# Moving the high and low parts of x from byte 288 to byte 384 of their 512-byte blocks in SBUF

## The chip, the cores and the metric

The kernel runs on one core of one Trainium2 chip. The metric is device time in microseconds (us), taken as the median of several runs; one further execution was recorded by the hardware profiler.

## What is computed

Two layers of a gated mixer over 256 rows of width 2048, in float32. Cut to what matters here:

```python
def _layer(x, norm_g, w_in, w_out):             # both layers have this frame
    h = matmul(_rmsnorm(x, norm_g), w_in)       # (256 x 2048) @ (2048 x 8192)
    q, k, v, z = split(h)
    y = attention(rope(q), rope(k), v) * silu(z)
    return x + matmul(y, w_out)                 # (256 x 2048) @ (2048 x 2048)

out = _rmsnorm(layer_1(layer_0(x)), final_norm)
```

Layer 0 uses dilated and differential attention, layer 1 block-sparse attention. Nearly all the work is in the four projections.

## The kernel before, in words

**Arithmetic.** Every float32 operand of a projection is held as two tiles of type float32r: a high part h (a copy by ScalarE) and a low part l = value - h (by VectorE). A product is then three matmuls, h*h, h*l and l*h. Each TensorE matmul is preceded by a load of its 128x128 stationary operand; the moving operand streams through with 256 or 512 columns.

**The tiles of x.** `xhl` (L63) is a list of 16 tiles, one for each 128 rows of the transposed activations. A tile is 128 partitions by 2048 bytes: 1024 bytes of high parts followed by 1024 bytes of low parts, 256 columns each. `split_x` (L159, writes at L162 and L163) fills it: once at the start from the input, and once after layer 0 from PSUM (`next_x`, L421).

**Where they lie.** Tiles are allocated one behind the other in SBUF, at the same byte offset in every partition. The pool `edge` comes first and begins 128 bytes past a multiple of 512. It holds a pad of PAD bytes, the 16 tiles of x (each a multiple of 512 bytes long), and a second pad of BACK bytes:

```python
    edge = ctx.enter_context(tc.tile_pool(name="edge", bufs=1))
    edge.tile([P, PAD // 4], F32, name="pad")
    xhl = [edge.tile([P, 2, S], F32R, name=f"x{i}") for i in range(KT)]
    edge.tile([P, BACK // 4], F32, name="pad2")
```

The pads are never read or written. With PAD = 160 every tile of x begins at 288 past a multiple of 512. PAD and BACK add up to 384, so all that is allocated behind begins at a multiple of 512: the weights' raw loads (`raw`), their split halves (`wh`, `wl`), the gated outputs (`yh`, `yl`), q, k, v and the rest. Every 128-column, 256-column or 512-column slice of a matmul operand in those tiles therefore begins at a multiple of 512, and every slice of x at 288 past one.

**The order of the work.** The loop at L505 goes through chunks, two layers of four groups and then the output projection. In a group the chunks q, k and z are 256 output columns wide, and v is 512 wide. It issues one matmul after another, and between them `fill` holds the attention steps for fixed slots. There are three forms of projection matmul:

- **q, k, z** (L529, L531): x is the moving operand and the weights are stationary. A pair is one matmul of 512 columns (high and low parts of x at once, against `wh`) and one of 256 columns (high part of x against `wl`).
- **v** (L523, through `mm3`, L312): x is the stationary operand, and `wh` or `wl` move with 512 columns.
- **output projection** (L523, through `mm3`, L312): `yh` or `yl` is stationary, and `wh` or `wl` move with 512 columns. No tile of x takes part.

```python
                        nc.tensor.matmul(ps[:, b], wh[ww][:, bs], xx, start=first, stop=False,
                                         skip_group_check=True)
                        nc.tensor.matmul(ps[:, b, 0:S], wl[ww][:, bs], xx[:, 0:S], start=False, stop=final,
                                         skip_group_check=True)
```

**The last chunk** (`last_chunk`, L443, matmuls at L462) is the last quarter of the output projection of layer 1. Four of its eight weight blocks were split into the tiles of x, which are free by then (L117 to L119), so there x tiles hold weights and move: with 512 columns for the first 128 rows, with 256 columns for the second 128 rows, against stationary `yh` and `yl`.

**Weights.** `load` (L91) brings a 1 MB raw block on SyncE's DMA queue; `split` (L111) makes `wh` on ScalarE (L133) and `wl` on VectorE (L134), some blocks ahead of their use.

Of the kernel before, what the change touches and what calls it, by code (L numbers as in the profile page):

```python
# [26 lines left out]
RAW_BUFS = 3  # L27
SPLIT_BUFS = 4
ALIGN = 512
PAD = 160  # L30
BACK = 224


def layer_chunks():
# [21 lines left out]
def trunk(ctx, tc, x_nat, x_t, w0, o0, w1, o1, g0, g1, gfin, lam, subln, cos_t, sin_t,  # L56
# [4 lines left out]
# [4 lines that stand above are left out]
    const = ctx.enter_context(tc.tile_pool(name="const", bufs=1))  # L65
# [569 lines left out]
```

## Time and profile before

| | |
|---|---|
| median of 3 runs | 958.21 us (958.12 to 958.51) |
| profiled execution, its own time | 958.89 us |
| its span, first to last instruction | 957.1 us |
| TensorE (PE) busy | 946.3 us, 99% of the span |
| weight loads (PEld) busy | 819.1 us, 86% |
| VectorE (DVE) busy | 639.3 us, 67% |
| ScalarE (ACT) busy | 526.3 us, 55% |
| HBM | 184 GB/s over the span |

PE is TensorE streaming a moving operand; PEld is the load of a stationary operand, which runs beside it. Matmuls are pipelined: the duration of one in the trace (about 390 ns for 512 columns) is longer than the time until the next one starts. What a matmul costs the kernel is the distance between starts, called its pitch here. It is read from the start times in the timeline, or from a stretch of uninterrupted matmuls divided by their number.

### The profile page before, as it was taken

To read this page: it belongs to the slowest core of one execution; us is meant where nothing else is said; L and a number is where in the kernel's file an instruction comes from. 1 tells how busy PE (TensorE), PEld (TensorE's weight loads), DVE (VectorE), ACT (ScalarE), POOL (GpSimd) and SP (SyncE) were. 2 spreads that over 40 slices of the span, in tenths; PEclk is the share of its full clock that TensorE was granted. 3 is DMA by queue.
4 is the path that set the end of the run, shared out by engine and by line. 5 is a ranking of instruction groups with operands and counts; after the bars stand their busy time and mean duration, and the time that the engine had idled before them with its cause. 6 is when DMAs were issued, how large, how long until landed. Compare 5 with 4: busy or idle time off the path is not lost.

```text
span 957.1 us, 13108 instructions
## 1 busy us (share of the span) xinstructions
PE 946.3 (99%) x5132; PEld 819.1 (86%) x5132; DVE 639.3 (67%) x973; ACT 526.3 (55%) x807; POOL 6.0 (1%) x12
## 2 busy tenths in 40 slices
PE   8999999999999999999999999999999999999996
PEld 7888888888888888888888898888889888888886
DVE  6778678557856785655566787685678567755572
ACT  7556556445645564454544665564566455644451
POOL 0000000000000000000000000000000000000000
PEclk9999999999999999999999999999999999999999
DMA  9775454445554554544555544545454545554542
GB/s 327 247 295 181 146 190 176 169 175 195 185 173 162 196 179 175 176 176 176 181 176 203 190 169 156 203 155 194 164 191 170 182 173 180 191 205 176 181 171 88
DMA packets 27854, 177.09 MB, mean 185 GB/s; under 512 B 3344, under 2 KB 4112, under 8 KB 7696
## 3 DMA queue, kind: packets, MB, share of 16 engines
q1 hardware_dynamic: 27504, 175.21, 51.5%
q10 hardware_dynamic: 288, 1.05, 0.4%
q8 instruction: 40, 0.66, 0.3%
q14 instruction: 22, 0.18, 0.1%
HBM read 174.15 MB, written 2.10 MB: 184 GB/s over the span
## 4 chain that ended last, share of the span: by engine, by line
PE 96%; issue 1%; DMA 1%; SPq 0%; ACT 0%; DVE 0%; POOL 0%; POOLq 0%; ACTq 0%
PE acc L529 36%; PE acc L312 34%; PE acc L531 19%; PE ps_s L312 1%; PE last L462 1%; PE ps_t L352 1%; DMA raw<-in_w 1%; PE po L312 1%; PE ps_s L317 1%; PE po L383 1%; PE pdo L312 0%; PE ps_xt L426 0%; PE ps_yt L409 0%; SPq L99 0%; SPq L150 0%
## 5 line engine op out<-in xcount | busy, mean ns | idle before, releaser
L134 DVE TENSOR_TENSOR wl<-raw,wh 128x1024 fp32r<-128x1024 f32 x314 | 384.3, 1224 | 244.7 <-ACT wh L133 242.2
L529 PE MATMUL acc<-x,wh 128*128 128x512 f32 x1536 | 541.1, 393 | 0.0
L133 ACT ACTIVATE wh<-raw 128x1024 fp32r<-128x1024 f32 x314 | 332.3, 1059 | 292.5 <-PE acc L529 138.4
L531 PE MATMUL acc<-x,wl 128*128 128x256 f32 x1536 | 432.8, 282 | 0.0
L529 PEld LDWEIGHTS acc<-x,wh 128*128 128x128 f32 x1536 | 288.5, 188 | 58.4
L531 PEld LDWEIGHTS acc<-x,wl 128*128 128x128 f32 x1536 | 290.2, 189 | 0.3
L312 PE MATMUL acc<-wh,x 128*128 128x512 f32 x512 | 164.8, 400 | 1.6 <-ACT wh L130 1.6
L312 PEld LDWEIGHTS acc<-wh,x 128*128 128x128 f32 x512 | 96.9, 189 | 24.8 <-ACT wh L130 1.8
L312 PE MATMUL acc<-wl,x 128*128 128x512 f32 x256 | 101.9, 398 | 0.5 <-DVE wl L134 0.2
L312 PE MATMUL acc<-wh,yh 128*128 128x512 f32 x224 | 88.4, 394 | 0.0
L312 PE MATMUL acc<-wh,yl 128*128 128x512 f32 x224 | 87.3, 390 | 0.0
L312 PE MATMUL acc<-wl,yh 128*128 128x512 f32 x224 | 87.2, 389 | 0.0
L312 PEld LDWEIGHTS acc<-wl,x 128*128 128x128 f32 x256 | 48.5, 190 | 12.6 <-DVE wl L134 0.7
L312 PEld LDWEIGHTS acc<-wh,yl 128*128 128x128 f32 x224 | 42.0, 188 | 9.0
L312 PEld LDWEIGHTS acc<-wl,yh 128*128 128x128 f32 x224 | 42.1, 188 | 8.3
L312 PEld LDWEIGHTS acc<-wh,yh 128*128 128x128 f32 x224 | 42.1, 188 | 8.3
L326 ACT ACTIVATE p<-p,st 128x128 f32<-128x128 f32 x64 | 28.5, 448 | 9.9 <-DVE st L322 9.6
L375 ACT ACTIVATE yh<-y 128x256 fp32r<-128x256 f32 x32 | 13.0, 417 | 34.4 <-DVE y L374 34.3
L290 DVE TENSOR_TENSOR rt<-rt,sr 128x512 f32<-128x512 f32 x32 | 22.1, 690 | 3.7 <-ACT rt L288 2.4
L287 ACT ACTIVATE rt<-rt 64x512 f32<-64x512 f32 x32 | 20.2, 631 | 7.7 <-DVE rt L286 7.0
L286 DVE TENSOR_TENSOR rt<-acc,rt 128x512 f32<-128x512 f32 x32 | 21.8, 683 | 0.1
L288 ACT ACTIVATE rt<-rt 64x512 f32<-64x512 f32 x32 | 20.2, 632 | 0.4
(131 smaller groups left out, 646.9 us busy)
## 6 DMA issues: line engine op xcount, KB each, us to landing
raw<-in_w SPq DMA_DIRECT2D x124, 1024.0 KB, 4.7
raw<-in_o SPq DMA_DIRECT2D x32, 1024.0 KB, 4.7
raw<-in_w SPq DMA_DIRECT2D x7, 512.0 KB, 8.7
xraw<-in_x_t SPq DMA_DIRECT2D x8, 256.0 KB, 7.7
x_sb<-in_x_nat SPq DMA_DIRECT2D x1, 2048.0 KB, 11.0
out<-x_sb SPq DMA_DIRECT2D x8, 256.0 KB, 2.5
gf<-in_gfin ACTq DMA_DIRECT2D x2, 512.0 KB, 4.5
raw<-in_w SPq DMA_DIRECT2D x2, 256.0 KB, 4.5
```

Source lines behind the costliest of these rows:

```text
L133: nc.scalar.activation(ht, r, AF.Copy)
L134: nc.vector.tensor_sub(lt, r, ht.bitcast(F32))
L286: nc.vector.tensor_add(t1, ps[:, :, 0:S], t1)
L287: nc.scalar.activation(t2[0:64], t1[64:128], AF.Copy)
L288: nc.scalar.activation(t2[64:128], t1[0:64], AF.Copy)
L290: nc.vector.tensor_mul(t2, t2, sr[:, None, :].to_broadcast([P, 2, S]))
L312: nc.tensor.matmul(out_, l, r, start=start and i == 0, stop=stop and i == 2)
L317: nc.tensor.matmul(ps[:, 0:P], q[:, h, 0:P], k[:, h, 0:P], start=True, stop=True)
L326: nc.scalar.activation(p[:, sl], p[:, sl], AF.Exp, bias=st[:, 0, i:i + 1], scale=-1.0, accum_out=st[:, 1, i:i + 1])
L375: nc.scalar.activation(yh[kt], y, AF.Copy)
L529: nc.tensor.matmul(ps[:, b], wh[ww][:, bs], xx, start=first, stop=False, skip_group_check=True)
L531: nc.tensor.matmul(ps[:, b, 0:S], wl[ww][:, bs], xx[:, 0:S], start=False, stop=final, skip_group_check=True)
```

## The change

The two pads change their sizes; their sum stays 384 bytes. The 16 tiles of x move up by 96 bytes, from 288 to 384 past a multiple of 512. Nothing else moves, and no instruction is added or removed.

```diff
 ALIGN = 512
-PAD = 160
-BACK = 224
+PAD = 256
+BACK = 128
```

## Rows read from the trace of the kernel before

**Rows 1.** The page: TensorE's busy time, and its granted clock in 40 slices.

```profile
PE 946.3 (99%) x5132; PEld 819.1 (86%) x5132; DVE 639.3 (67%) x973; ACT 526.3 (55%) x807; POOL 6.0 (1%) x12
...
PEclk9999999999999999999999999999999999999999
```

**Rows 2.** The page: the chain that ended last, by engine.

```profile
PE 96%; issue 1%; DMA 1%; SPq 0%; ACT 0%; DVE 0%; POOL 0%; POOLq 0%; ACTq 0%
```

**Rows 3.** What TensorE waited for: us in total, times, longest us.

```profile
PE acc L312 <- ACT wh L130: 1.6, 1, 1.6
PE pw L148 <- DVE fs L450: 1.1, 1, 1.1
PE acc L312 <- DVE wl L134: 0.2, 1, 0.2
```

**Rows 4.** Costliest groups: line, engine, operation, out<-in, shapes, xcount | busy us, mean ns | idle before.

```profile
L529 PE MATMUL acc<-x,wh 128*128 128x512 f32 x1536 | 541.1, 393 | 0.0
L531 PE MATMUL acc<-x,wl 128*128 128x256 f32 x1536 | 432.8, 282 | 0.0
L312 PE MATMUL acc<-wh,x 128*128 128x512 f32 x512 | 164.8, 400 | 1.6 <-ACT wh L130 1.6
L312 PE MATMUL acc<-wl,x 128*128 128x512 f32 x256 | 101.9, 398 | 0.5 <-DVE wl L134 0.2
...
L133 ACT ACTIVATE wh<-raw 128x1024 fp32r<-128x1024 f32 x314 | 332.3, 1059 | 292.5 <-PE acc L529 138.4
```

**Rows 5.** Chain that ended last, in order of time: start us, us, what. v chunks, then output projection.

```profile
15.08 16.83 PE acc L312 x71
...
269.93 22.40 PE acc L312 x96
...
440.82 4.13 PE acc L312 x18
...
873.91 53.08 PE acc L312 x234
```

**Rows 6.** Timeline of PE, q/k/z just after a v chunk, then settled: start us, us, instruction.

```profile
292.16 0.40 PE L529 MATMUL acc<-x,wh 128*128 128x512 f32 x1
292.40 0.28 PE L531 MATMUL acc<-x,wl 128*128 128x256 f32 x1
292.51 0.40 PE L529 MATMUL acc<-x,wh 128*128 128x512 f32 x1
...
293.22 0.39 PE L529 MATMUL acc<-x,wh 128*128 128x512 f32 x1
...
300.18 0.39 PE L529 MATMUL acc<-x,wh 128*128 128x512 f32 x1
300.41 0.28 PE L531 MATMUL acc<-x,wl 128*128 128x256 f32 x1
...
302.26 0.39 PE L529 MATMUL acc<-x,wh 128*128 128x512 f32 x1
```

**Rows 7.** Timeline of PE in the last chunk: x tiles moving, then wh and wl moving.

```profile
929.62 0.63 PE L462 MATMUL last<-x,yh 128*128 128x512 f32 x2
...
931.02 0.63 PE L462 MATMUL last<-x,yh 128*128 128x512 f32 x2
...
938.25 0.40 PE L462 MATMUL last<-x,yh 128*128 128x256 f32 x2
...
939.30 0.39 PE L462 MATMUL last<-x,yh 128*128 128x256 f32 x2
...
942.02 0.28 PE L462 MATMUL last<-wh,yl 128*128 128x256 f32 x1
...
943.10 0.28 PE L462 MATMUL last<-wh,yl 128*128 128x256 f32 x1
```

**Rows 8.** Line L162, ScalarE's writes into the x tiles: duration ns min/median/max, first and last start.

```profile
L162 ACT ACTIVATE x<-xraw,g_sb x16: 489/495/509, 3.8 to 21.7; 128x256 fp32r<-128x256 f32 x16
L162 ACT ACTIVATE x<-ps_xt,g_sb x16: 458/474/476, 418.7 to 492.1; 128x256 fp32r<-128x256 f32 x16
```

## The prediction

> **What bounds the kernel now.** I read the page first, for who is busy: TensorE 99% of the span, at full granted clock in all 40 slices (2.4 GHz) [rows 1]. Then the chain that ended last: 96% of it is TensorE [rows 2]. Then what TensorE waited for: about 3 us in all, none of it after the start [rows 3]. So the kernel is a row of matmuls without gaps, and its time is the sum of their pitches, the distances between starts. Whatever the change does to a pitch reaches the end one for one; whatever it does to another engine is worth nothing as long as that engine keeps ahead, and ScalarE sat idle 292.5 us before its weight splits, most of it waiting for TensorE [rows 4].
>
> The pitch is therefore what to read, by the position of x. At 2.4 GHz 512 columns alone would stream in 213.3 ns and 256 in 106.7 ns. All operands but the tiles of x begin at multiples of 512 bytes, so the trace before already holds matmuls with x and without it:
>
> - **x stationary, weights moving, 512 columns (v).** One whole v chunk is 96 matmuls in 22.40 us, 233.3 ns each [rows 5].
> - **No x, 512 columns (output projection).** 234 matmuls in 53.08 us, 226.8 ns each; the short piece of 18 in 4.13 us gives 229.4, since the first few after an interruption are slower [rows 5].
> - **x moving, 512 columns, alone (last chunk).** Six starts in 1.40 us (929.62 to 931.02), 233.3 ns each [rows 7].
> - **x moving, 256 columns, alone (last chunk).** Nine in 1.05 us, 116.7 ns each; with `wh`, `wl` moving nine take 1.08 us, 120.0 ns each [rows 7].
> - **x moving in pairs of 512 and 256 (q, k, z).** Six pairs from 300.18 to 302.26, 346.7 ns a pair, split as 0.23 and 0.12 [rows 6]. Just after a v chunk a pair takes longer: three from 292.16 to 293.22 are 353.3 ns each, and then it settles [rows 6].
>
> So the same shape costs 233.3 ns where one operand is an x tile, on either side, and 226.8 ns where both operands begin at a multiple of 512: 6.5 ns more for 213.3 ns of columns. In the pairs that cost does not show: 346.7 is the sum of the two forms without x, 226.8 + 120.0 = 346.8. A pitch thus depends on where the operands begin, and it can sit at a slow value or settle to a fast one.
>
> **The change part by part.** Only the start of the 16 x tiles moves, from 288 to 384. Instructions, order, waits, DMAs and all other addresses stay. No matmul, semaphore or queue entry is added or taken away.
>
> *v, 768 matmuls (512 + 256 in [rows 4]).* No row has a tile at 384. The nearest from below is the output projection, 226.8 ns; from above today's 233.3 ns; a value still worse is bounded by the slowest steady row of this shape, 233.3 too. I take 226.8: 288 is a multiple of 32 only, while 384 is a multiple of 128 as is every start of the fast form, and the likeliest cause of 6.5 ns at 288 is a read that starts off such a boundary. Seven chunks run without a gap: 672 x 6.5 = 4.4 us. The first chunk is held by its loads until 15.08; from there 71 matmuls take 16.83 us, 237.0 ns each [rows 5], which gives up to 71 x 6.5 = 0.5 us and perhaps nothing. I take 4.5 us saved for v, with ends 0 and 4.9.
>
> *q, k, z, 1536 pairs [rows 4].* Here x moves. The nearest row for an aligned pair is the sum of the aligned forms, 346.8 ns against 346.7: I take no change. Below, a pair could reach 226.8 + 116.7 = 343.5 (the 256-column part at its best), 1536 x 3.2 ns = 4.9 us saved; above, 353.3, the pair just after a v chunk, 1536 x 6.6 ns = 10.1 us lost. This is the largest unknown: one nanosecond a pair is 1.5 us.
>
> *Last chunk.* 24 matmuls of 512 columns would gain 24 x 6.5 = 0.16 us, 48 of 256 columns would lose up to 48 x 3.3 = 0.16 us: nothing.
>
> *Writes into the x tiles.* 32 on ScalarE at 458 to 509 ns [rows 8], as many on VectorE. If a write at 384 took 5% more or less, 25 ns, it would stay hidden behind the matmuls, which run on; without that cover 64 x 25 ns = 1.6 us. Zero.
>
> The sum is 4.5 us. The profiled execution took 958.89 us, 957.1 of it in the span; less 4.5 it would be 954.4. It stands 0.7 us above the median of 958.21, to which the forecast refers: **953.7 us**, its own range 952.5 to 955.5. A measurement of this kernel can tell about 0.2%, 1.9 us, from no change.
>
> **The rivals.**
>
> *Pairs lose their fast rhythm (slower).* The pairs at 288 take 346.7 ns although a lone 512-column matmul with x moving at 288 takes 233.3 [rows 7]; so 288 may be a favourable offset for moving x, in which the weight load beside it and the moving stream don't get in each other's way, and 384 may not be. Then every pair would stay at the 353.3 ns with which they begin after v: 10.1 us more by the sum above. With v's gain of 4.5 the time is 963.8 us; without it 968.3. It decides from 2.9 ns a pair, where it has eaten v's 4.5 us. For it: the slow rhythm exists in this trace at unchanged addresses, and the 256-column matmul is faster with x at 288 (116.7) than aligned (120.0). Against it: the aligned forms settle at 226.8 and 120.0, which add to no more than today's pair.
>
> *Nothing changes.* v stays at 233.3 if what counts is the distance from a multiple of 512 or 256, of which 384 is none; pairs stay at 346.7. Or the address does not matter, and v is slower than the output projection for another reason. 958.2 us. Reads that go by small pieces would give this as well: both positions are multiples of 32. The pads are whole multiples of 32 with an unchanged sum, so that the tiles fail to move is improbable, and would give the same time.
>
> The Trainium skill ("SBUF — State Buffer", Specifications) gives SBUF 16-byte cachelines; 288 and 384 are both multiples of 16, and by that alone the change does nothing, 958.2 us. The skill ("TensorE: Matmul & The Clock Gate", Part 2, step 4) also says that the streaming operand and the weight load have independent read ports, which speaks against a slowdown by the weights' position. Here the trace does not agree: stationary x costs 6.5 ns more than stationary y under equal moving operands [rows 5].
>
> *Both gain.* v as forecast, and the 256-column part keeps 116.7 ns: 343.5 ns a pair, another 4.9 us, 948.8 us. For it only the short row of the last chunk [rows 7].
>
> **How the numbers follow.** Forecast 0.38; pairs lose their rhythm 0.36, of which 0.22 with v's gain (963.8) and 0.14 without (968.3); nothing changes 0.20; both gain 0.06. The predicted time is the forecast's, 953.7. Faster by over 0.2% is forecast and "both gain": 0.44; within 0.2% 0.20; slower 0.36. The range leaves out "both gain" below and 968.3 above, 0.20 together: 951.0 to 964.5. Both signs hold much of the chance, so 952.5 to 955.5 is the range of the likeliest case alone.
>
> **What would show it.** In the chain that ended last each v chunk of 96 would take 21.8 us instead of 22.40, the output projection's 234 still 53.1. The timeline in q, k, z should show pairs 346.7 ns apart, from the first pair after v on. A pair at 350 ns or more throughout, or one settling near 353, shows the slower rival; v pieces at 22.40 show that 384 is for stationary x what 288 was. TensorE's waits should stay at about 3 us and the clock at full; if either moved, the argument from pitches would be wrong altogether, and so would it if the output projection, whose tiles don't move, changed its 226.8 ns.

## The result and the profile after

With the x tiles at 384 the kernel takes 963.59 us (963.36 to 963.83) against 958.34 us for the kernel before in the same comparison: ratio 1.0055, 95% interval 1.0038 to 1.0072. It is 5.25 us slower. The profiled execution took 963.36 us with a span of 961.6 us, against 958.89 and 957.1.

The page of the kernel after shows the engines' busy time. TensorE's matmuls have grown by 5.0 us (946.3 in [rows 1]) and its weight loads by 1.3; the other engines stay within 0.3 us. The granted clock was 0.996 of 2.4 GHz over the profiled execution, as before.

```profile
PE 951.3 (99%) x5132; PEld 820.4 (85%) x5132; DVE 639.6 (67%) x973; ACT 526.0 (55%) x807; POOL 6.0 (1%) x12
```

The next rows list what TensorE waited for after the change: us in total, times, longest. It is the same start-up as in [rows 3], so the time did not come in as a wait:

```profile
PE acc L312 <- ACT wh L130: 1.4, 1, 1.4
PE pw L148 <- DVE fs L450: 1.1, 1, 1.1
PE acc L312 <- DVE wl L131: 0.2, 1, 0.2
```

The costliest groups after (line, engine, operation, out<-in, shapes, count | busy us, mean ns). Against [rows 4] the two forms of q, k, z have grown, by 5.6 and 1.3 us of busy time, and the two of v have hardly moved:

```profile
L529 PE MATMUL acc<-x,wh 128*128 128x512 f32 x1536 | 546.7, 396 | 0.0
...
L531 PE MATMUL acc<-x,wl 128*128 128x256 f32 x1536 | 434.1, 283 | 0.0
...
L312 PE MATMUL acc<-wh,x 128*128 128x512 f32 x512 | 164.3, 399 | 1.4 <-ACT wh L130 1.4
...
L312 PE MATMUL acc<-wl,x 128*128 128x512 f32 x256 | 101.8, 397 | 0.2 <-DVE wl L131 0.2
```

The timeline of TensorE after is taken in q, k, z well away from any v chunk (start us, us, instruction). Six pairs take 2.11 us, 351.7 ns each, where [rows 6] have 346.7:

```profile
299.69 0.39 PE L529 MATMUL acc<-x,wh 128*128 128x512 f32 x1
299.92 0.28 PE L531 MATMUL acc<-x,wl 128*128 128x256 f32 x1
300.04 0.39 PE L529 MATMUL acc<-x,wh 128*128 128x512 f32 x1
300.27 0.28 PE L531 MATMUL acc<-x,wl 128*128 128x256 f32 x1
300.39 0.40 PE L529 MATMUL acc<-x,wh 128*128 128x512 f32 x1
300.62 0.28 PE L531 MATMUL acc<-x,wl 128*128 128x256 f32 x1
300.74 0.40 PE L529 MATMUL acc<-x,wh 128*128 128x512 f32 x1
...
301.80 0.40 PE L529 MATMUL acc<-x,wh 128*128 128x512 f32 x1
```

The chain that ended last, after the change and in order of time, shows a v chunk and then the long piece of the output projection. v is 22.32 / 96 = 232.5 ns a matmul instead of 233.3; the output projection keeps its 53.08 us of [rows 5] to the digit.

```profile
271.22 22.32 PE acc L312 x96
...
878.31 53.08 PE acc L312 x234
```

Over the whole trace a pitch is taken here as the mean distance between one start and the next of the same stage; the few of 300 ns and more (47 of some 1,500 among the pairs) are left out, and a pair's pitch is the sum of those of its two parts. Before: pairs 347.1 ns, v 233.3, output projection 227.4. After: pairs 350.8, v 232.5, output projection 227.4. Then 1536 x 3.7 = 5.7 us lost in the pairs, 768 x 0.8 = 0.6 us gained in v: 5.1 us, against 5.25 measured.

### The profile page after: what moved, and what is told of

Same layout as the page of the kernel before. It is cut to its first block, busy times and chain, and to the rows that moved or that the text cites. A ratio compares the mean times of both kernels' runs of the same rounds, so it can differ in the third digit from the quotient of the medians.

```text
span 961.6 us, 13108 instructions
## 1 busy us (share of the span) xinstructions
PE 951.3 (99%) x5132; PEld 820.4 (85%) x5132; DVE 639.6 (67%) x973; ACT 526.0 (55%) x807; POOL 6.0 (1%) x12
## 4 chain that ended last, share of the span: by engine, by line
PE 97%; issue 1%; DMA 0%; ACT 0%; DVE 0%; POOL 0%; SPq 0%; POOLq 0%; ACTq 0%
PE acc L529 37%; PE acc L312 35%; PE acc L531 19%; PE ps_s L312 1%; PE last L462 1%; PE ps_t L352 1%; PE po L312 1%; PE ps_s L317 1%; PE po L383 1%; PE pdo L312 0%; DMA raw<-in_w 0%; PE ps_xt L426 0%; PE ps_yt L409 0%; POOL fs L480 0%; PE pr L237 0%
## 5 line engine op out<-in xcount | busy, mean ns | idle before, releaser
L529 PE MATMUL acc<-x,wh 128*128 128x512 f32 x1536 | 546.7, 396 | 0.0
```

## The experiments

Groups 1 to 4 change only where operands begin; group 5 changes the order of matmuls, and group 6 the tiles of the weights and the room around them. The edits are shown against the kernel before, cut to what matters. "Distance" is the start of an x tile less the start of the weights' split halves.

**1. Is it the position of x, or its distance from the weights?** Two kernels set one against the other.

```diff
-PAD = 160
-BACK = 224
+PAD = 256     # both_up96: x at 384, all else at 96, distance 288
+BACK = 224
```

> x at 384 as after the change, and everything else moved up by the same 96 bytes, so that x again lies 288 past the weights' start modulo 512. Theory R (what counts is the distance between the starts of the moving and the stationary operand, modulo 512): the kernel before in every pitch, pairs in q, k, z 346.7 ns, v 233.3 ns, output projection 226.8 ns, time 958.3 us. Theory A (what counts is where the x tile itself begins): the pairs stay as after the change, about 351 ns, and the time at about 963.6 us, with the output projection perhaps slower as its tiles have left the multiples of 512.

958.58 us, ratio to the kernel before 1.0001 (0.9991 to 1.0010): the whole loss is gone although x is at 384. Timeline of that kernel, six pairs in 2.08 us, 346.7 ns each:

```profile
300.14 0.39 PE L529 MATMUL acc<-x,wh 128*128 128x512 f32 x1
...
302.22 0.39 PE L529 MATMUL acc<-x,wh 128*128 128x512 f32 x1
```

```diff
-BACK = 224
+BACK = 128    # weights_down96: x at 288, all else at 416, distance 384
```

> x stays at 288, everything else is moved down by 96 bytes to 416, so that x lies 384 past the weights' start modulo 512. Theory R: the kernel after the change in every pitch, pairs about 351 ns, v 232.4 ns, output projection 226.8 ns, time 963.6 us. Theory A: the pairs of before, 346.7 ns, and about 958.3 us, but for what the weights lose by leaving the multiples of 512.

963.83 us, ratio 1.0054 (1.0039 to 1.0069), pairs 350.8 ns, v 232.5, output projection 227.4: the kernel after the change, with x where it was before. Theory A, by which x's own position counts, falls; the distance decides.

**2. The position that the forecast had in mind: everything level.**

```diff
-PAD = 160
-BACK = 224
+PAD = 384     # x_at_0: x at 0, all else at 0
+BACK = 0
```

> x and everything else at multiples of 512. Both theories: v falls to the output projection's 226.8 ns, 768 x 6.5 ns = 4 to 5 us saved against 288. If a pair is the sum of the two aligned forms, 226.8 + 120.0 = 346.8 ns, the time is 953.7 us. If pairs without an offset lose their rhythm as at 384 (351 ns or more), it is 960 us or more.

961.81 us, ratio 1.0035 (1.0022 to 1.0048). The chain in order of time shows that v does fall to the output projection's pitch, 21.77 / 96 = 226.8 ns:

```profile
271.97 21.77 PE acc L312 x96
...
877.90 53.08 PE acc L312 x234
```

But a pair takes longer than in the settled stretches above. The timeline of the same kernel has six pairs in 2.12 us, 353.3 ns each (352.1 over the whole trace); the 256-column part takes 0.11 to 0.12 us, and the 512-column part 0.23 to 0.24. The pairs do settle, but into a cycle of three that repeats: two of 350 ns and one of 360, 1.06 us together:

```profile
299.94 0.40 PE L529 MATMUL acc<-x,wh 128*128 128x512 f32 x1
300.18 0.28 PE L531 MATMUL acc<-x,wl 128*128 128x256 f32 x1
300.29 0.40 PE L529 MATMUL acc<-x,wh 128*128 128x512 f32 x1
...
300.65 0.40 PE L529 MATMUL acc<-x,wh 128*128 128x512 f32 x1
...
301.00 0.40 PE L529 MATMUL acc<-x,wh 128*128 128x512 f32 x1
...
301.35 0.40 PE L529 MATMUL acc<-x,wh 128*128 128x512 f32 x1
...
301.71 0.40 PE L529 MATMUL acc<-x,wh 128*128 128x512 f32 x1
...
302.06 0.40 PE L529 MATMUL acc<-x,wh 128*128 128x512 f32 x1
```

So v gains 768 x 6.1 = 4.7 us, and the pairs lose 1536 x 5.0 = 7.7 us.

```diff
-PAD = 160
-BACK = 224
+PAD = 256     # all_at_384: x at 384, all else at 384, distance 0
+BACK = 0
```

> x and everything else at 384 past a multiple of 512. Theory R: every pitch as with everything at 0, within half a nanosecond, and the same time within 0.2%. Theory A: v stays at 232 to 233 ns and the pairs near 351 ns as after the change, and the output projection leaves 226.8 ns.

961.92 us, ratio 1.0035 (1.0022 to 1.0047), pairs 352.1, v 227.3, output projection 227.4 ns. Its chain has the v chunk of x_at_0 to the digit:

```profile
270.81 21.77 PE acc L312 x96
```

Level at 384 is the same as level at 0. Nor does an operand need to begin at a multiple of 128: in both_up96 the operands of the output projection begin at 96, and its pitch is 227.4 ns all the same. What counts is the distance of the operands from each other.

**3. The map of distances.** The same two constants, other values (PAD and BACK of r32: 0, 480; r96: 0, 416; r160: 32, 352; r192: 64, 320; r224: 96, 288; r256: 128, 256; r320: 192, 192).

> x 32 bytes past the weights' start modulo 512 (288 before, 384 after). Theory H (half way: the pairs are fast when the moving x is about half of 512 bytes away from the weights' start): slow pairs, 351 ns or more, 962 us or more. Theory S (small pieces: a start 32 bytes past a multiple of 64 is what the pairs need, and 288, not 384, has it): pairs 346.7 ns as before, and 958.5 us. In both v stays above the 227.2 ns that it has only without an offset.

> x 256 bytes past the weights' start modulo 512. Theory H: pairs 346.7 ns or less, 958.5 us or less. Theory S: 256 is a multiple of 64, so slow pairs as at 0 and 384, 351 to 352 ns, and 962 us or more, or with v at 227 ns some 961.8 us.

> x 320 bytes past the weights' start modulo 512, between the 288 of before and the 384 of after. Theory H: pairs between 346.7 and 350.8 ns, time between 958.5 and 963.6 us. Theory S: 320 is a multiple of 64, so pairs at 351 ns or more, 963 us or more.

> x 224 bytes past the weights' start modulo 512, as far below 256 as 288 is above. Theory H: pairs near 346.7 ns, 958 to 959 us. Theory S: 224 is 32 past a multiple of 64, so 346.7 ns too and 958.5 us; this run tells the two apart only with the other three, and shows whether the sign of the distance matters.

> x 96 bytes past the weights' start. With a period of 256 (0 and 256 gave equal pitches, and so did 32 and 288), 96 is one of the three distances not yet seen. Theory S (32 past a multiple of 64 is good for the pairs) is wrong already at 224; if only 32 itself is good, pairs are 350 to 352.5 ns here, v 232 to 233.5 ns, and the time 963 to 966 us.

> x 160 bytes past the weights' start, another distance not yet seen. If only 32 is good for the pairs: 350 to 352.5 ns, v 232 to 233.5 ns, 963 to 966 us. If there is a second good distance, pairs of 347.1 ns or less and 958.5 us or less.

> x 192 bytes past the weights' start, the last of the eight distances modulo 256 in steps of 32. If only 32 and 160 are good for the pairs: 350 to 352.5 ns, v 232 to 234 ns, 963 to 966 us. If good distances are those 128 apart (32 and 160), 192 goes with 64: 351.7 ns, v 233.3 ns, 965.4 us.

Pitches in ns and times in us; a distance of 256 or more is set in its line modulo 256:

```
distance  pair   v      output  time (kernels)
0         352.1  227.2  227.4   961.81, 961.92; at 256: 961.37
32        347.1  233.3  227.4   958.50; at 288: 958.58, and the kernel before
64        351.7  233.3  227.4   at 320: 965.37
96        350.4  234.2  227.4   964.50
128       350.8  232.5  227.4   at 384: 963.83, and the kernel after, 963.59
160       347.1  233.3  227.4   958.91
192       353.0  229.0  227.4   964.57
224       352.4  233.3  227.4   966.01
```

Distances 256 apart gave the same pitches, twice: 0 and 256, 32 and 288. For the other distances the period is not shown; 64 and 128 were run only as 320 and 384. 128 apart did not (0 and 128 differ by 5 ns in v, 64 and 192 by 4). Theory H falls, since 32 and 160 are the good ones and 256 is not; theory S falls at 96 and 224, though both good distances are 32 past a multiple of 128. Each stage has its own favourite: the pairs 32 and 160, v only 0. The kernel before sits on a distance that is best for the pairs and poor for v; the change moved it to one that is poor for both.

**4. With what does a stream collide?** Low and high parts of the weights were put 32 bytes apart modulo 256, with yh and yl moved along, by changing their order and putting a small tile between them. In w_low32 x is level with the high parts, in w_high32 with the low parts:

```diff
+            lt = wpool.tile([P, 2 * CW], F32R, tag="wl", name=f"wl{m}")
+            if m == 0:
+                wpool.tile([P, GAP // 4], F32, tag="gap", name="gap", bufs=1)
             ht = wpool.tile([P, 2 * CW], F32R, tag="wh", name=f"wh{m}")
-            lt = wpool.tile([P, 2 * CW], F32R, tag="wl", name=f"wl{m}")
```

PAD, BACK, GAP are 0, 224, 32 in w_low32 and 0, 0, 224 in w_high32.

> x level with the high parts of the weights modulo 256, and 32 bytes past their low parts; yh lies level with wh, and yl with wl. Theory C (a moving stream collides with the load of the next stationary operand, which runs beside it): the 512-column matmul of a pair streams x while wl is loaded (distance 32), the 256-column one while wh is loaded (distance 0); the output projection streams wh while yh is loaded and wl while yl is loaded, all at distance 0, so it keeps 227.4 ns; v has distance 0 in two of three matmuls, so between 227 and 231 ns; if the 512-column part decides, the pair keeps 347 ns and the time is 955 to 957 us. Theory O (a matmul's stream against its own stationary operand): two of three matmuls of the output projection come to distance 32, which makes it 230 ns or more and the kernel slower than 958.5 us by some 2 us, less what v gains.

> The other way about: x level with the low parts of the weights and 32 past their high parts, yh level with wh and yl with wl. Theory C: the 512-column matmul of a pair is at distance 0, the 256-column one at 32; if the 512-column part decides, pairs of 351 to 352 ns as at distance 0, and 961 us or more; output projection 227.4 ns; v with one matmul of three at distance 0, 229 to 232 ns. Theory O: the output projection at 230 ns or more as in the run with the low parts shifted.

w_low32 took 969.10 us (ratio 1.0111, 1.0094 to 1.0128) and w_high32 963.47 us (1.0053, 1.0038 to 1.0068). Pairs, v and output projection had pitches of 352.5, 232.6 and 231.6 ns in the first and 348.2, 233.2 and 232.0 in the second. In w_low32 the long piece of the output projection itself became slow, 54.21 / 234 = 231.7 ns instead of 226.8:

```profile
882.92 54.21 PE acc L315 x234
```

That refutes theory C (a stream against the next stationary operand), which had all its distances at 0 there; if the 512-column part decides, it also had the pairs the wrong way round, 347 ns in w_low32 and 351 or more in w_high32. Theory O (a stream against its own stationary operand) foresaw the slower output projection, and each kernel's pairs come within 1.1 ns of those of the table at x's distance from wh, the 512-column part's own stationary operand: 352.1 at 0, 347.1 at 32. But by theory O alone one matmul in three of the output projection (wh against yh, level) should have kept 227 ns, and its mean distance is 231.8 ns. So neither pairing by itself is the rule: what came just before counts too. These runs do not tell whether that is an offset between successive streams or the slow settling that group 5 shows, and whether reads inside TensorE collide at all is left open.

**5. Is it the alternation of lengths?** At distance 0 the lone forms are at their best and the alternating pair is not. The same matmuls were issued in another order: four of 512 columns, then their four of 256 (g4, its edit below), or eight and eight over two slots of the loop (g8).

```diff
-            for i in range(per):
+            for part in range(1 if w == CW else 2):
+                for i in range(per):
...
-                        nc.tensor.matmul(ps[:, b], wh[ww][:, bs], xx, start=first, stop=False,
-                                         skip_group_check=True)
-                        nc.tensor.matmul(ps[:, b, 0:S], wl[ww][:, bs], xx[:, 0:S], start=False, stop=final,
-                                         skip_group_check=True)
+                            if part == 0:
+                                nc.tensor.matmul(ps[:, b], wh[ww][:, bs], xx, start=first, stop=False,
+                                                 skip_group_check=True)
+                            else:
+                                nc.tensor.matmul(ps[:, b, 0:S], wl[ww][:, bs], xx[:, 0:S], start=False,
+                                                 stop=final, skip_group_check=True)
```

> Everything at multiples of 512 (distance 0), and in q, k, z the order is four matmuls of 512 columns, then the four of 256 that belong to them, instead of one and one. Theory L (at distance 0 a row of equal matmuls has the lone pitch, 226.7 ns for 512 columns and 120.0 ns for 256, and it is the alternation that costs 5 ns a pair): 346.7 ns a pair and a little at each of the changes, 347 to 349 ns, v 227.4 ns, 954 to 957 us. Theory M (pairs at distance 0 are slow for another reason than their alternation): 352 ns a pair on average, 961.8 us.

> Distance 0 with eight matmuls of 512 columns and then eight of 256. Theory L: half the changes of the four-and-four order, so nearer to 346.7 ns a pair, 953.5 to 956 us. Theory M: 352 ns, 961.8 us.

> The kernel before with the same regrouping, four and four. Theory L: the forms fall back to their lone pitches at 288, 233.5 and 117.4 ns, 351 ns a pair, and the time rises to some 964 us. Theory M: the pairs stay at 347.1 ns, 958.5 us.

Measured: 958.88 us at distance 0 in fours, 957.42 in eights, 963.32 at 288 in fours, against 961.81 and 958.49 with the old order. At 0 regrouping saves 2.9 and 4.4 us; at 288 it costs 4.8 us, and the pieces take 233 and 117 ns, near the lone pitches of 288. That is theory L's direction in all three and M's in none, but g4 missed its range and g8 too: 954 to 957 and 953.5 to 956 were expected. The chain of g8 in order of time shows eight matmuls of 512 columns in 1.84 us, 230 ns each, and eight of 256 in 0.95 us:

```profile
213.86 1.84 PE acc L529 x8
215.70 0.95 PE acc L532 x8
216.66 1.84 PE acc L529 x8
218.50 0.95 PE acc L532 x8
```

The distances between the starts of two such rounds of g8, in ns, show where the rest goes:

```
512: 233 236 229 232 231 227 226 227   256: 113 119 120 120 120 120 120 120
512: 234 236 228 232 231 227 227 226   256: 114 119 120 120 120 120 120 120
```

After 256 columns five matmuls of 512 run slow before the row settles at 226.7 ns; after 512 columns two of 256 run short before the row settles at 120.0. The means over all undisturbed rounds of g8 agree with these within 1 ns. A round so costs 349.1 ns a pair instead of the lone forms' 346.7. One and one, the pairs of distance 0 settle too, but into their cycle of 350, 350 and 360 ns and not at the lone pitches.

**6. Each stage at its own distance.** x is put 32 past the weights for the pairs, and for v alone the halves of the weights are written 32 bytes further on in their tiles, so that v is level. Room was made by sharing one tile between the two masks, the second loaded later, and giving y one buffer; PAD is 0. The edit is cut to the lines on v:

```diff
-            ht = wpool.tile([P, 2 * CW], F32R, tag="wh", name=f"wh{m}")
-            lt = wpool.tile([P, 2 * CW], F32R, tag="wl", name=f"wl{m}")
+            ht = wpool.tile([P, 2 * CW + 64], F32R, tag="wh", name=f"wh{m}")
+            lt = wpool.tile([P, 2 * CW + 64], F32R, tag="wl", name=f"wl{m}")
             w = wide[m // 2]
+            off = OFF if is_v[m // 2] else 0      # OFF = 8 columns, 32 bytes
+            ht, lt = ht[:, off:off + 2 * CW], lt[:, off:off + 2 * CW]
```

> x 32 bytes past the weights' start in q, k, z, where that is good, and level with them in v: the halves of v's weights are written 32 bytes further on in their tiles. To make room the two masks share one tile and y has one buffer. If pitches follow the distance of each stage's own operands: pairs 347.1 ns, v 227.4 instead of 233.3 ns, output projection 227.4 ns, and 4 to 4.5 us saved against the kernel before, 954.0 to 954.7 us. If the shared mask or the single y delays the splits, TensorE waits for them and some of it is lost.

954.16 us (953.91 to 954.45), ratio 0.9956 (0.9942 to 0.9969): faster than both kernels. A v chunk now takes 21.80 us, the output projection its 53.08:

```profile
174.56 21.80 PE acc L320 x96
...
868.78 53.08 PE acc L320 x234
```

and the pairs keep 346.7 ns (six from 290.24 to 292.32, 2.08 us):

```profile
290.24 0.39 PE L537 MATMUL acc<-x,wh 128*128 128x512 f32 x1
...
292.32 0.39 PE L537 MATMUL acc<-x,wh 128*128 128x512 f32 x1
```

Its counter-test sets OFF to 0 and keeps all else.

> The version with v level, with its 32-byte step taken back to nothing and all else kept (larger weight tiles, shared mask, one y buffer). If the step alone made the 4.3 us: pairs 347.1 ns, v 233.3 ns, 958.5 us. If the larger tiles or the rest had a share in it, the time stays below 958 us.

958.61 us, ratio 1.0000 (0.9991 to 1.0009), v back at 233.3 ns. So the 32 bytes in v's tiles are worth the 4.3 us, and the room made for them neither costs nor gives anything.

## Why the prediction was wrong

- **What bounds the kernel** held. TensorE's waits and clock did not move, no other engine changed, and the pitches account for 5.1 of the 5.25 us.
- **The term for v failed.** The prediction took 226.8 ns for v at 384, on the ground that 384, like every start of the fast form, is a multiple of 128. v went to 232.5 and gave 0.6 us, not 4.5. The row that v was compared with, the output projection, was fast because both of its operands were level modulo 256, not because they were at multiples of 512: all_at_384 is as fast. With level operands v does take 226.8 ns (x_at_0), so the size of the prize was right and the condition for it wrong. "What counts is the distance from a multiple of 512 or 256", in the rival of no change, was nearer, though it is a distance between two operands.
- **The term for the pairs failed**, and it cost the most: the prediction set it at no change, and it came to 5.7 us. The prediction added two lone forms, 226.8 + 120.0, to find an aligned pair, got 346.8 and took the match with today's 346.7 as its reason to expect no change. A level pair takes 352.1 ns, a pair at 384 took 350.8; the match was a coincidence. The trace before held a warning: at 288 the lone forms are 233.3 and 116.7 [rows 7], 350.0 together, and the alternating pair took 346.7 [rows 6]. Sums of lone forms were 3 ns off there already; the prediction noted it and used the sum all the same. The regrouped kernels show that the alternation itself sets the pitch: in rows of four and eight the forms move towards their lone pitches, which makes the kernel faster at distance 0 and slower at 288. The alternating pairs settle into a rhythm of their own, 346.7 ns at 288 and a cycle of three at 0.
- **The rival "pairs lose their fast rhythm"** is what happened, in direction and place. Its price came out close, 963.8 against 963.59, by two errors that cancel: pairs rose by 3.7 ns instead of 6.6, since they settled into a new rhythm that differs from the 353.3 of the starts after v, and v gained next to nothing, 0.6 us instead of 4.5. The prediction's wide range, 951.0 to 964.5, holds the measured 963.59 us by this rival alone.
- **The last chunk** was rightly set at nothing. With x moving at 512 columns six starts still take 1.40 us, 233.3 ns; at 256 columns the nine now take 1.08 us, 120.0 ns instead of 116.7 [rows 7]:

```profile
932.62 0.63 PE L462 MATMUL last<-x,yh 128*128 128x512 f32 x2
...
934.02 0.63 PE L462 MATMUL last<-x,yh 128*128 128x512 f32 x2
...
942.63 0.40 PE L462 MATMUL last<-x,yh 128*128 128x256 f32 x2
...
943.71 0.40 PE L462 MATMUL last<-x,yh 128*128 128x256 f32 x2
```

- **What the Trainium skill says.** Steps of 32 bytes, whole multiples of the 16 bytes that the Trainium skill ("SBUF — State Buffer", Specifications) gives for a cacheline, moved the time by up to 7.5 us (958.50 at distance 32, 966.01 at 224). The Trainium skill ("TensorE: Matmul & The Clock Gate", Part 2, step 4) says that the streaming operand and the weight load have independent read ports. Taken as a promise that the two reads never disturb each other, that does not fit either: v's pitch went from 227.2 to 234.2 ns with nothing but the starts of its operands changed (x_at_0 and r96).

## What to carry to other kernels

Where TensorE has no gaps, read pitches from start times, by stage, and, for matmuls like these, ask of each stage how far its operands begin from each other modulo 256 bytes; a good value for one order of matmuls can be a poor one for the next, and a few bytes inside the tiles of one stage can serve both. Do not put the pitch of a mixed sequence together from the pitches of uniform ones: measure the sequence itself. A sweep of eight kernels that differ in two constants gave the map in steps of 32 bytes.

## What had not been expected of the hardware

For float32r matmuls with a weight load each, the pitch depended on the distance between operand starts modulo 256 bytes and not on the absolute position: kernels with equal distances agreed within 0.2 ns in the mean pitches of pairs, v and output projection (x_at_0 and all_at_384; the kernel before, both_up96 and r32). Over the distances tried 512 columns in v took 227.2 to 234.2 ns, and a pair of 512 and 256 columns 347.1 to 353.0. At distance 0, a row of 512 columns after one of 256 needed five matmuls to settle, and alternating pairs fell into a cycle of three (350, 350 and 360 ns). Why the distance acts at all, and why 32 and 160 suit the pairs, no run here settles.
